# Layer 1's rows divided by their norm on ScalarE, then turned by plain transposes instead of by products with a diagonal

## The chip, the cores and the metric

The kernel runs on one core of one Trainium2 chip. The metric is the device time of one execution in microseconds (us). The median of three runs of the kernel before is 1140.3 us.

## The reference

Two residual layers act on 256 rows of width 2048. Layer 0 mixes with a gated spatial unit, layer 1 with latent attention. Both begin alike, and the change concerns how layer 1 begins:

```python
def rms_norm(x, g):
    xf = x.astype(jnp.float32)
    y = xf * lax.rsqrt(jnp.mean(xf * xf, axis=-1, keepdims=True) + NORM_EPS)
    return (y * g.astype(jnp.float32)).astype(x.dtype)
...
def reference(x, c, ada_w, ada_b, pre_g, post_g, sgu_w_in, ...):
    cond = jax.nn.silu(c)
    for i in range(DEPTH):                                  # DEPTH = 2
        mod = cond @ ada_w[i] + ada_b[i]
        shift, scale, gate = jnp.split(mod, 3, axis=-1)
        h = rms_norm(x, pre_g[i]) * (1 + scale[:, None, :]) + shift[:, None, :]
        ...
        y = sgu_mixer(h, ...) if i % N_MIXERS == 0 else mla_mixer(h, ...)   # both start with h @ w_in
        x = x + gate[:, None, :] * rms_norm(y, post_g[i])
    return x
```

Everything is float32.

## The kernel before

**Tiling.** The 256 rows are two blocks of 128, `b = 0` and `b = 1`; a block's 2048 columns are four tiles `q = 0..3` of 128 x 512. TensorE (PE) contracts over partitions, so the left operand of each product is a turned 128 x 128 piece (16 pieces, index `k`, four in each `q`). A float32 product is made of three: every operand is split into a rounded high part (`...H`, or `h` of a weight) and a remainder (`...L`, `l`), and PE sums high x high, low x high and high x low. ScalarE (ACT) makes the high part with a cast, VectorE (DVE) the low part with a subtraction. Weights stream in as tiles of 128 x 2 x 512 (`wm_0`, `wm_2`, ... for layer 1's input weights; a number is the first `k` of two), cast to `wm_..h` by ACT and subtracted to `wm_..l` by DVE.

**Order.** Each engine takes its instructions in the order in which the Python code writes them. Around the joint of the two layers this order is written out by hand in the string `PLAN`.

**The joint.** Layer 0's last matrix `po` ends with column tile 3, block 0 ahead of block 1. When block 0's sums are done, `ready1` adds the residual to the four tiles (`add`, DVE, tiles named `yg` in the trace, `x1[b][q]` in the code), squares and sums them (ACT), takes the root (ACT, tile `r`), its reciprocal (DVE, `ri`), and multiplies the identity matrix by that column: `d`, a diagonal with each row's 1/norm (DVE, `diag_of`, line 273). `turn_h1` then multiplies each 128 x 128 piece of `x1` with that diagonal on PE, which turns the piece and scales it in one product. For block 1 the same six steps lie in the list `later`, and the plan's `c1` runs one of them at a time.

**The plan's letters.** `Tbq` is `turn_h1` (four pieces into two PSUM banks, tile `h`), `Fbq` is `mod_h1` (two pieces by ACT, two by DVE: times `amul`, plus `shift`, tile `h1f`), `Hbq` the two casts to `h1H` on ACT, `Lbq` the two subtractions to `h1L` on DVE. `gN` issues N weight tiles' products for block 0, `bN` for block 1, `eN` N of layer 0's last ones (block 1), `s1` stages one weight tile (cast and subtraction), `c1` one step of `later`. The part that matters here:

```python
PLAN = "e1 e1 e1 e1 T00 T01 s1 F00 F01 H00 L00 H01 e1 e1 L01 T02 T03 g1 c1 F02 H02 c1 g1 g1 L02 s1 c1 c1 g1 c1 F03
        c1 g1 H03 g1 L03 T11 s1 T10 F11 F10 H10 L10 g1 s1 b1 H11 b1 L11 T12 F12 H12 L12 s1 T13 b1 F13 H13 ..."
```

So block 0's last `ready1` step stands just ahead of `e1 e1 e1 e1` in the code (ACT and DVE have no work in these), and block 1's last one (the sixth `c1`) between `F03` and `H03`. The four PSUM banks of the pool `pa` hold two `T` at a time, so `T02` and `T03` take the banks that `F00` and `F01` have read.

Of the kernel before, what the change touches and what calls it, by code (L numbers as in the profile page):

```python
# [8 lines left out]
F32 = mybir.dt.float32  # L9
# [6 lines left out]
P = 128  # L16
D = 2048
KD = D // P
S = 256
NB = S // P  # L20
# [134 lines left out]
def tile_trunk(  # L155
# [7 lines left out]
    nc = tc.nc  # L163
    x = x[0]
    out = out[0]
# [5 lines left out]
    sp = ctx.enter_context(tc.tile_pool(name="sp", bufs=1))  # L171
# [6 lines left out]
    def slot(name, shape=(P, 512), dt=F32):  # L178
        return sp.tile(list(shape), dt, tag="s", name=name, bufs=SLOTS)

    def small(name, n):
        return sp.tile([P, n], F32, tag="sm", name=name, bufs=16)
# [4 lines left out]
    def aux_bank(name):  # L187
        return pa.tile([P, 512], F32, tag="ax", name=name)

    def mm(o, l, r, start, stop):  # L190
        nc.tensor.matmul(o, lhsT=l, rhs=r, start=start, stop=stop)  # L191
# [12 lines left out]
    ident = const.tile([P, P], F32, name="ident")  # L204
# [49 lines left out]
    def rstd_of(ss, n, name, between=None):  # L254
        r = small(name, 1)
        nc.scalar.activation(r, ss, AF.Sqrt, bias=eps_t, scale=1.0 / n)
        if between:
            between()
        ri = small(name + "i", 1)
        nc.vector.reciprocal(out=ri, in_=r)  # L260
        return ri

    def sumsq(parts, name):
# [3 lines left out]
        t = small(name + "t", 1)  # L267
        nc.vector.reduce_sum(out=t, in_=ss, axis=AX.X)
        return t

    def diag_of(r, name):
        d = sp.tile([P, P], F32, tag="diag", name=name, bufs=4)
        nc.vector.tensor_scalar_mul(d, ident, r)
        return d


    def ada_items(name, src, width, state):
# [144 lines left out]
    def chunk_tasks(name, ks, lhs, evac, per=2):  # L422

        ps = [None, None]
        tasks = []
        ks = list(ks)
        for i in range(0, len(ks), per):
            def task(b, g, i=i):
                if i == 0:
                    ps[b] = acc_bank(f"{name}_{b}")  # L430
                h, l = g
                for j, k in enumerate(ks[i:i + per]):
                    xh, xl = lhs(k, b)
                    f = i + j == 0
                    e = i + j == len(ks) - 1
                    wh, wl = (h[j], l[j]) if isinstance(h, list) else (h[:, j, :], l[:, j, :])
                    mm(ps[b], xh, wh, f, False)
                    mm(ps[b], xl, wh, False, False)
                    mm(ps[b], xh, wl, False, e)
                if i + per >= len(ks):  # L440
                    evac(b, ps[b])

            tasks.append((lambda g, t=task: t(0, g), lambda g, t=task: t(1, g)))
        return tasks
# [288 lines left out]
    def visit(n, k0, nk):  # L733
        last = k0 + nk == KD
        ev = ev_first(n) if k0 == 0 else ev_add(n, None if not last else on_u if n < 8 else on_v)
        return chunk_tasks(f"pi_{n}_{k0}", range(k0, k0 + nk), lhs0, ev)
# [64 lines left out]
    for j, (n, k0, nk, _) in enumerate(rest):  # L801
        t = visit(n, k0, nk)
# [14 lines left out]
    def ev_z(j):  # L817
        def evac(b, ps):
            def f():
                z = slot(f"z_{j}_{b}")  # L820
                u = part[j, b]
                nc.scalar.activation(z, ps, AF.Silu)
                nc.vector.tensor_tensor(out=u, in0=u, in1=z, op=ALU.mult)
                ready.append((j, b))
            deferred.append(f)
        return evac
# [12 lines left out]
    for j in range(8):  # L839
        t = chunk_tasks(f"piz_{j}", range(KD), lhs0, ev_z(j))  # L840
# [33 lines left out]
    def ev_out(l, n, done):  # L874
        def evac(b, ps):
            def f():
                if n == 0:
                    ssy[l][b] = small(f"ssy_{l}_{b}", 4)
                nc.scalar.activation(junk, ps, AF.Square, accum_out=ssy[l][b][:, n:n + 1])
                yg[l][b][n] = slot(f"yg_{l}_{n}_{b}")  # L880
                if gates[l][n] is None:
                    nc.scalar.copy(out=yg[l][b][n], in_=ps)
                    unscaled.append((b, n))
                    return

                def gate():
                    nc.vector.tensor_tensor(out=yg[l][b][n], in0=ps, in1=gates[l][n], op=ALU.mult)

                if n < 3:
                    gate()  # L890
                else:
                    done(b, gate)

            if n == 3:
                f()
            else:
                deferred.append(f)
        return evac

    def y_rstd(l, b, gate):  # L900
        t = small(f"sst_{l}_{b}", 1)
        nc.vector.reduce_sum(out=t, in_=ssy[l][b], axis=AX.X)
        return rstd_of(t, D, f"ry_{l}_{b}", gate)

    x1 = yg[0]
    dg1 = [None, None]

    later = []

    def ready1(b, gate):  # L910
        r, ss1 = [], small(f"ss1_{b}", 4)

        def norm():
            r.append(y_rstd(0, b, gate))

        def add(q):
            y = yg[0][b][q]
            nc.vector.scalar_tensor_tensor(y, y, r[0], xr[b][q], op0=ALU.mult, op1=ALU.add)
            nc.scalar.activation(junk, y, AF.Square, accum_out=ss1[:, q:q + 1])

        def turn():
            t = small(f"ss1t_{b}", 1)
            nc.vector.reduce_sum(out=t, in_=ss1, axis=AX.X)
            dg1[b] = diag_of(rstd_of(t, D, f"r1_{b}"), f"d1_{b}")

        steps = [norm] + [lambda q=q: add(q) for q in range(4)] + [turn]
        if b == 0:
            for f in steps:
                f()
        else:  # L930
            later.extend(steps)

    lhs_y = quad_lhs(yH, yL)
    for n in range(4):
        t = chunk_tasks(f"po_{n}", range(32), lhs_y, ev_out(0, n, ready1))
# [17 lines left out]
    def turn_h1(b, q):  # L953
        ps = hp1[b][q] = [aux_bank(f"h1_{b}_{q}_{i}") for i in range(2)]
        for i in range(4):
            mm(ps[i // 2][:, (i % 2) * P:(i % 2 + 1) * P], x1[b][q][:, i * P:(i + 1) * P], dg1[b], True, True)

    def mod_h1(b, q):
        ps = hp1[b][q]
# [29 lines left out]
    def ev_lat(n):  # L989
        def evac(b, ps):  # L990
            def f():
                lat[b][n] = slot(f"lat_{b}_{n}")
                nc.scalar.copy(out=lat[b][n], in_=ps)
            deferred.append(f)
        return evac

    t = chunk_tasks("pm_0", range(KD), lhs1, ev_lat(0))
# [21 lines left out]
    def tail(n):  # L1019
        for f in later[:n]:  # L1020
            f()
        del later[:n]

    acts = dict(T=turn_h1, F=mod_h1, H=high_h1, L=low_h1)
    for w in PLAN.split():
        if w[0] in "THFL":
# [84 lines left out]
    def ev_sz(n):  # L1111
        def evac(b, ps):
            def f():
                sz[b][n] = slot(f"sz_{b}_{n}")
                nc.scalar.activation(sz[b][n], ps, AF.Silu)
            deferred.append(f)
        return evac

    t = chunk_tasks("pm_2", range(KD), lhs1, ev_sz(0))
# [5 lines left out]
    t = chunk_tasks("pm_3", range(KD), lhs1, ev_sz(1))  # L1125
# [245 lines left out]
    t = chunk_tasks("pp_2", range(KD), lhs_o, ev_out(1, 2, finish))  # L1371
# [3 lines left out]
    t = chunk_tasks("pp_3", range(KD), lhs_o, ev_out(1, 3, finish))  # L1375
# [51 lines left out]
```

## Time and profile before

| what | value |
|---|---|
| time, median of 3 runs | 1140.3 us (1138.54 to 1141.61) |
| profiled execution | 1140.05 us |
| its span, first to last instruction | 1138.3 us |
| PE busy | 1109.9 us, 98% of the span |
| DVE busy | 901.6 us, 79% |
| ACT busy | 571.3 us, 50% |
| mean granted TensorE clock | 0.998 |

The profile shows one execution, and its times of day are us from the start of the span. The profiled execution took 1.75 us more than its span. The work that changes lies between 766 us and 791 us. "Idle before" in a row is the time in which the engine did nothing ahead of this instruction, with the engine and tile that ended it. A duration of the profile reaches past the start of the next instruction of the same engine, where the two overlap; from start to start is then what one costs in a row of them.

### The profile page before, as it was taken

What the parts mean: (1) busy time and instruction counts of PE and PEld (TensorE: products, weight loads), DVE (VectorE), ACT (ScalarE), POOL (GpSimd) and SP (SyncE); (2) the same over time, 40 slices, a digit from 0 to 9 for tenths busy, and PEclk for the clock granted to TensorE, in tenths of its full rate; (3) what the DMA queues carried; (4) which work ended last, traced back from release to release, by engine and by line L of the source; (5) the groups of instructions that cost most, each with busy time, mean ns of one, the idle gap of its engine ahead of it and who ended that gap; (6) DMA issues with size and microseconds to landing.
All of it is one profiled execution on the core that took longest, in us unless ns stands there. A gap on an engine that the chain in (4) does not pass through costs nothing.

```text
span 1138.3 us, 15632 instructions
## 1 busy us (share of the span) xinstructions
PE 1109.9 (98%) x5585; PEld 940.3 (83%) x5585; DVE 901.6 (79%) x1201; ACT 571.3 (50%) x821; POOL 23.8 (2%) x51
## 2 busy tenths in 40 slices
PE   5999999999999999999999999999999999999997
PEld 4787878888887888888888888888888999999885
DVE  3889899978888898898788788857888467568765
ACT  3765434354456555554544443457574445455441
POOL 1000000000000000000001000000000000000000
PEclk9999999999999999999999999999999999999999
DMA  9999898988786987788689999973988445345672
GB/s 325 316 323 321 280 369 289 366 286 279 250 296 227 313 308 241 258 273 292 231 299 333 362 365 354 385 235 93 354 309 277 146 153 169 92 148 187 229 280 82
DMA packets 158206, 304.34 MB, mean 267 GB/s; under 512 B 12057, under 2 KB 29056, under 8 KB 158128
## 3 DMA queue, kind: packets, MB, share of 16 engines
q1 hardware_dynamic: 156128, 297.84, 76.5%
q0 software_dynamic: 1968, 5.49, 1.7%
q8 instruction: 44, 0.72, 0.2%
q14 instruction: 34, 0.28, 0.1%
q10 hardware_dynamic: 32, 0.01, 0.0%
HBM read 301.17 MB, written 2.11 MB: 266 GB/s over the span
## 4 chain that ended last, share of the span: by engine, by line
PE 81%; DVE 7%; DMA 5%; ACT 4%; issue 3%; SPq 0%; DVEq 0%; ACTq 0%
PE pi L191 18%; PE piz L191 15%; PE po L191 15%; PE pm L191 10%; PE pp L191 8%; DMA wi<-in_sgu_w_in_dram 3%; PE k L191 2%; PE v L191 2%; PE s L191 2%; PE qn L191 2%; PE o L191 1%; DMA first<-in_ada_w_dram 1%; PE mix L191 1%; DVE part L702 1%; PE qr L191 1%
## 5 line engine op out<-in xcount | busy, mean ns | idle before, releaser
L296 DVE SCALAR_TENSOR_TENSOR acc_ada<-ada,sc,acc_ada 128x1024 f32<-128x1024 f32 (+1 forms) x135 | 148.8, 1102 | 0.8
L296 DVE SCALAR_TENSOR_TENSOR acc_gate<-gate,sc,acc_gate 128x1024 f32<-128x1024 f32 x60 | 76.7, 1278 | 0.0
L702 DVE TENSOR_TENSOR part<-pi,part 128x512 f32<-128x512 f32 x92 | 59.2, 683 | 1.2 <-PE pi L191 1.2
L113 ACT CAST wi_8h<-wi 128x1024 fp32r<-128x1024 f32 x24 | 25.2, 1051 | 36.5 <-DMA wi<-in_sgu_w_in_dram 30.5
L113 ACT CAST wi_6h<-wi 128x1024 fp32r<-128x1024 f32 x24 | 25.1, 1051 | 36.4 <-DMA wi<-in_sgu_w_in_dram 30.3
L113 ACT CAST wi_4h<-wi 128x1024 fp32r<-128x1024 f32 x24 | 25.2, 1051 | 28.2 <-DMA wi<-in_sgu_w_in_dram 26.9
L114 DVE TENSOR_TENSOR wi_10l<-wi,wi_10h 128x1024 fp32r<-128x1024 f32 x24 | 29.3, 1221 | 12.1 <-ACT wi_10h L113 11.9
L114 DVE TENSOR_TENSOR wi_14l<-wi,wi_14h 128x1024 fp32r<-128x1024 f32 x24 | 29.3, 1221 | 7.0 <-ACT wi_14h L113 7.0
L114 DVE TENSOR_TENSOR wi_6l<-wi,wi_6h 128x1024 fp32r<-128x1024 f32 x24 | 29.3, 1220 | 4.2 <-ACT wi_6h L113 4.2
L114 DVE TENSOR_TENSOR wi_8l<-wi,wi_8h 128x1024 fp32r<-128x1024 f32 x24 | 29.3, 1221 | 3.8 <-ACT wi_8h L113 3.8
L114 DVE TENSOR_TENSOR wi_0l<-wi,wi_0h 128x1024 fp32r<-128x1024 f32 x23 | 28.1, 1221 | 5.2 <-ACT wi_0h L113 5.2
L114 DVE TENSOR_TENSOR wi_12l<-wi,wi_12h 128x1024 fp32r<-128x1024 f32 x24 | 29.3, 1220 | 2.7 <-ACT wi_12h L113 2.5
L114 DVE TENSOR_TENSOR wi_4l<-wi,wi_4h 128x1024 fp32r<-128x1024 f32 x24 | 29.3, 1220 | 2.1 <-ACT wi_4h L113 2.1
L113 ACT CAST wi_2h<-wi 128x1024 fp32r<-128x1024 f32 x24 | 25.2, 1051 | 11.3 <-DMA wi<-in_sgu_w_in_dram 9.2
L1271 ACT ACTIVATE sm<-sm,nm 128x128 f32<-128x128 f32 (+1 forms) x32 | 14.3, 448 | 32.4 <-DVE nm L1269 32.3
L113 ACT CAST wi_10h<-wi 128x1024 fp32r<-128x1024 f32 x24 | 25.1, 1045 | 10.8 <-DMA wi<-in_sgu_w_in_dram 10.1
L114 DVE TENSOR_TENSOR wi_2l<-wi,wi_2h 128x1024 fp32r<-128x1024 f32 x24 | 29.3, 1221 | 1.2 <-ACT wi_2h L113 1.2
L113 ACT CAST wi_0h<-wi 128x1024 fp32r<-128x1024 f32 x23 | 24.1, 1050 | 10.5 <-DMA wi<-in_sgu_w_in_dram 9.3
L113 ACT CAST wi_12h<-wi 128x1024 fp32r<-128x1024 f32 x24 | 25.2, 1049 | 5.5 <-DMA wi<-in_sgu_w_in_dram 3.6
L113 ACT CAST wi_14h<-wi 128x1024 fp32r<-128x1024 f32 x24 | 25.1, 1045 | 4.7 <-PE pi L191 2.5
L715 ACT ACTIVATE part<-part 128x512 f32<-128x512 f32 x16 | 9.9, 632 | 34.7 <-DVE part L702 34.7
L191 PE MATMUL pi<-wi_4h,hH 128*128 128x512 f32 x64 | 25.3, 396 | 1.1 <-DVE part L702 1.1
(694 smaller groups left out, 3811.1 us busy)
## 6 DMA issues: line engine op xcount, KB each, us to landing
wi<-in_sgu_w_in_dram SPq DMA_DIRECT2D x191, 512.0 KB, 5.3
ada<-in_ada_w_dram SPq DMA_DIRECT2D x240, 256.0 KB, 5.3
gate<-in_ada_w_dram SPq DMA_DIRECT2D x64, 512.0 KB, 5.4
wo<-in_sgu_w_out_dram SPq DMA_DIRECT2D x64, 512.0 KB, 6.2
wm<-in_mla_w_in_dram SPq DMA_DIRECT2D x48, 512.0 KB, 5.5
wp<-in_mla_w_out_dram SPq DMA_DIRECT2D x32, 512.0 KB, 5.3
ukv<-in_mla_w_ukv_dram SPq DMA_DIRECT2D x16, 512.0 KB, 4.6
uq<-in_mla_w_uq_dram SPq DMA_DIRECT2D x12, 384.0 KB, 3.2
```

Of the source, the lines that this page charges most:

```text
L113: self.nc.scalar.copy(out=h, in_=raw)
L114: self.nc.vector.tensor_tensor(out=l[0:rows], in0=raw[0:rows], in1=h[0:rows].bitcast(F32), op=ALU.subtract)
L191: nc.tensor.matmul(o, lhsT=l, rhs=r, start=start, stop=stop)
L296: nc.vector.scalar_tensor_tensor(acc, raw, w, acc, op0=ALU.mult, op1=ALU.add)
L702: nc.vector.tensor_tensor(out=part[n, b], in0=ps, in1=part[n, b], op=ALU.add)
L715: nc.scalar.activation(part[n, b], part[n, b], AF.Gelu)
L1271: nc.scalar.activation(sm[:, i, :], sm[:, i, :], AF.Exp, bias=nm[:, i:i + 1], scale=scale, accum_out=su[:, i:i + 1])
```

## The change

The diagonal goes. In its place ACT multiplies each of the block's four tiles `x1[b][q]` (128 x 512) by the column `ri` and writes the result to a tile of its own, `x1n[b][q]`. `turn_h1` then turns the pieces of `x1n` with PE's transpose, against the identity. For block 0 the four are written in the order 0, 1, 2, 3, for block 1 in the order 1, 0, 2, 3, which is that of `T11`, `T10`, `T12`, `T13`. `x1` itself stays as it is, since the end of the kernel adds it again. The eight new tiles come from the same pool of 53 slots as most others.

```diff
-    def diag_of(r, name):
-        d = sp.tile([P, P], F32, tag="diag", name=name, bufs=4)
-        nc.vector.tensor_scalar_mul(d, ident, r)
-        return d
...
-    dg1 = [None, None]
+
+    x1n = [[None] * 4 for _ in range(NB)]
...
         def turn():
             t = small(f"ss1t_{b}", 1)
             nc.vector.reduce_sum(out=t, in_=ss1, axis=AX.X)
-            dg1[b] = diag_of(rstd_of(t, D, f"r1_{b}"), f"d1_{b}")
+            ri = rstd_of(t, D, f"r1_{b}")
+            for q in (0, 1, 2, 3) if b == 0 else (1, 0, 2, 3):
+                x1n[b][q] = slot(f"x1n_{b}_{q}")
+                nc.scalar.mul(x1n[b][q], x1[b][q], ri)
...
     def turn_h1(b, q):
         ps = hp1[b][q] = [aux_bank(f"h1_{b}_{q}_{i}") for i in range(2)]
         for i in range(4):
-            mm(ps[i // 2][:, (i % 2) * P:(i % 2 + 1) * P], x1[b][q][:, i * P:(i + 1) * P], dg1[b], True, True)
+            nc.tensor.transpose(out=ps[i // 2][:, (i % 2) * P:(i % 2 + 1) * P],
+                                in_=x1n[b][q][:, i * P:(i + 1) * P], identity=ident)
```

**ACT's queue at the end of block 0's norm.** In the rows that follow, the digits after a tile's name are its indices (`b`, `q` and, for `h1f`, the half) and a running number; a tile's own trailing digit before the first underscore is dropped. Before:

```order
L256 ACTIVATE r_0_6652<-ss1t_6650,eps_t 128x1
L113 CAST wm_8h<-wm_8_6554 128x1024
L965 ACTIVATE h1f_0_0_6707<-h_0_0_0_6689,shift,amul 128x128 x2
L965 ACTIVATE h1f_1_0_6713<-h_0_1_0_6695,shift,amul 128x128 x2
L975 CAST h1H_0_6719<-h1f_0_0_6707 128x256
```

And with the change:

```order
L256 ACTIVATE r_0_6652<-ss1t_6650,eps_t 128x1
L923 ACTIVATE x1n_0_6656<-yg_0_0_5620,r_0i 128x512
L923 ACTIVATE x1n_1_6658<-yg_1_0_5983,r_0i 128x512
L923 ACTIVATE x1n_2_6660<-yg_2_0_6336,r_0i 128x512
L923 ACTIVATE x1n_3_6662<-yg_3_0_6633,r_0i 128x512
L113 CAST wm_8h<-wm_8_6554 128x1024
L965 ACTIVATE h1f_0_0_6713<-h_0_0_0_6695,shift,amul 128x128 x2
L965 ACTIVATE h1f_1_0_6719<-h_0_1_0_6701,shift,amul 128x128 x2
L975 CAST h1H_0_6725<-h1f_0_0_6713 128x256
```

All four products stand ahead of the cast of `wm_8` and of everything that ACT does for `F00`, `F01`, `H00` and `H01`.

**ACT's queue at the end of block 1's norm.** The same place for block 1, the sixth `c1` of the plan. Before:

```order
L965 ACTIVATE h1f_3_0_6816<-h_0_3_0_6752,shift,amul 128x128 x2
L256 ACTIVATE r_1_6824<-ss1t_6822,eps_t 128x1
L975 CAST h1H_3_6836<-h1f_3_0_6816 128x256
L975 CAST h1H_3_6836<-h1f_3_1_6817 128x256
L113 CAST wm_12h<-wm_12_6568 128x1024
L965 ACTIVATE h1f_1_0_6866<-h_1_1_0_6848,shift,amul 128x128 x2
L965 ACTIVATE h1f_0_0_6872<-h_1_0_0_6860,shift,amul 128x128 x2
```

And with the change:

```order
L965 ACTIVATE h1f_3_0_6822<-h_0_3_0_6758,shift,amul 128x128 x2
L256 ACTIVATE r_1_6830<-ss1t_6828,eps_t 128x1
L923 ACTIVATE x1n_1_6834<-yg_1_1_5986,r_1i 128x512
L923 ACTIVATE x1n_0_6836<-yg_0_1_5624,r_1i 128x512
L923 ACTIVATE x1n_2_6838<-yg_2_1_6339,r_1i 128x512
L923 ACTIVATE x1n_3_6840<-yg_3_1_6747,r_1i 128x512
L975 CAST h1H_3_6848<-h1f_3_0_6822 128x256
L975 CAST h1H_3_6848<-h1f_3_1_6823 128x256
L113 CAST wm_12h<-wm_12_6568 128x1024
L965 ACTIVATE h1f_1_0_6878<-h_1_1_0_6860,shift,amul 128x128 x2
```

Here the casts of `h1H` for block 0's last tile and of `wm_12` move behind the four products. The order of PE's instructions is the same before and after; only what its 32 turning instructions read differs. DVE loses its two `d` and keeps its order otherwise.

## Rows read from the trace of the kernel before

**Rows 1.** Page, part 1: busy time, share of the span, instructions, by engine.

```profile
PE 1109.9 (98%) x5585; PEld 940.3 (83%) x5585; DVE 901.6 (79%) x1201; ACT 571.3 (50%) x821; POOL 23.8 (2%) x51
```

**Rows 2.** Windows view to PE's end: busy PE, PEld, DVE, ACT, POOL; granted clock; DMA.

```profile
797.00:1130.00 333.00, 331.41 (x1996) 294.40 (x1994) 232.50 (x394) 168.35 (x287) 5.61 (x9) 1.00 0.61 204
```

**Rows 3.** Timeline of PE (start, us, what, idle before) at the joint.

```profile
767.29 2.02 PE L191 MATMUL h<-d,yg 128*128 128x128 f32 x16
769.07 0.48 PE L191 MATMUL po<-wo_28h,yH 128*128 128x512 f32 x1
...
771.92 1.95 PE L191 MATMUL h<-d,yg 128*128 128x128 f32 x16
773.62 0.48 PE L191 MATMUL pm<-wm_0h,h1H 128*128 128x512 f32 x1
...
782.35 2.05 PE L191 MATMUL h<-d,yg 128*128 128x128 f32 x16 [0.31 <-DVE d L273]
...
786.25 0.50 PE L191 MATMUL pm<-wm_0h,h1L 128*128 128x512 f32 x1 [0.19 <-DVE h1L L981]
...
788.88 1.95 PE L191 MATMUL h<-d,yg 128*128 128x128 f32 x16
790.58 0.48 PE L191 MATMUL pm<-wm_4h,h1H 128*128 128x512 f32 x1
```

**Rows 4.** Timeline of PE: eight plain transposes of layer 0.

```profile
426.87 1.03 PE L834 MATMUL yt<-ident,part 128*128 128x128 f32 x8
427.65 0.47 PE L191 MATMUL piz<-wi_4h,hH 128*128 128x512 f32 x1
```

**Rows 5.** Timeline of ACT: the same product on layer 0's rows, line 551.

```profile
21.02 0.70 ACT L551 ACTIVATE x<-x,rx_0i 128x512 f32<-128x512 f32 x1
21.63 0.71 ACT L551 ACTIVATE x<-x,rx_1i 128x512 f32<-128x512 f32 x1
```

**Rows 6.** Timeline of ACT at the joint.

```profile
766.53 1.04 ACT L113 CAST wm_8h<-wm 128x1024 fp32r<-128x1024 f32 x1
...
778.66 0.63 ACT L919 ACTIVATE junk<-yg 128x512 bf16<-128x512 f32 x1 [2.01 <-DVE yg L918]
...
781.49 0.29 ACT L256 ACTIVATE r<-ss1t,eps_t 128x1 f32<-128x1 f32 x1
781.67 0.70 ACT L975 CAST h1H<-h1f 128x256 fp32r<-128x256 f32 x2
782.28 1.05 ACT L113 CAST wm_12h<-wm 128x1024 fp32r<-128x1024 f32 x1
```

**Rows 7.** Timeline of DVE at the joint.

```profile
766.65 0.17 DVE L260 RECIPROCAL r_0i<-r 128x1 f32<-128x1 f32 x1 [0.36 <-ACT r L256]
...
768.74 1.36 DVE L968 TENSOR_SCALAR h1f<-h,amul,shift 128x128 f32<-128x128 f32 x4
770.04 1.43 DVE L981 TENSOR_TENSOR h1L<-h1f,h1H 128x256 fp32r<-128x256 f32 x4
772.84 0.16 DVE L902 TENSOR_REDUCE sst<-ssy 128x1 f32<-128x4 f32 x1 [1.37 <-ACT junk L879]
...
776.68 1.22 DVE L114 TENSOR_TENSOR wm_10l<-wm,wm_10h 128x1024 fp32r<-128x1024 f32 x1 [1.06 <-ACT wm_10h L113]
...
781.81 0.17 DVE L260 RECIPROCAL r_1i<-r 128x1 f32<-128x1 f32 x1 [0.72 <-ACT r L256]
...
783.36 1.23 DVE L114 TENSOR_TENSOR wm_12l<-wm,wm_12h 128x1024 fp32r<-128x1024 f32 x1 [0.39 <-ACT wm_12h L113]
...
785.78 0.98 DVE L981 TENSOR_TENSOR h1L<-h1f,h1H 128x256 fp32r<-128x256 f32 x2
```

**Rows 8.** Timeline of PE: two successive wide products shortly after PE's sparse first stretch.

```profile
31.28 0.58 PE L191 MATMUL pi<-wi_firsth,hH 128*128 128x512 f32 x1
31.69 0.40 PE L191 MATMUL pi<-wi_firsth,hL 128*128 128x512 f32 x1
```

**Rows 9.** Windows view: a stretch after PE's last product (columns as in rows 2).

```profile
1134.00:1135.00 1.00, 0.00 (x0) 0.00 (x0) 0.53 (x1) 0.00 (x0) 0.00 (x0) 0.59 0.93 350
```

## Prediction

> **What bounds the kernel now.** I read the page first, then PE's timeline at the joint of the layers, then those of ACT and DVE beside it. PE is busy for 98% of the span [rows 1], and from 797 us to its end it is idle for 1.6 us of 333 us [rows 2]. So a microsecond of PE time saved or lost at the joint reaches the end nearly whole: nothing behind the joint has slack to swallow it, and none of PE's waits there is for a transfer. What the reader must then see is who leads at the joint itself. For block 0 it is PE: its products with the diagonal at 767.29 and 771.92 start without a wait [rows 3]. For block 1 it is the chain of ACT and DVE: PE waits 0.31 us for `d` at 782.35 and again 0.19 us for `h1L` at 786.25 [rows 3]. That chain has no slack at these two points, and the change adds work to it.
>
> **What PE saves.** The 16 records from 767.29 to 769.07 are eight products with a diagonal: 1.78 us [rows 3]. The same count takes 1.70 us from 771.92 to 773.62 and from 788.88 to 790.58 [rows 3]. Eight plain transposes take 0.78 us from their start to that of the next product [rows 4]. So a pair of `T` becomes 0.92 to 1.0 us shorter, and the four pairs some 3.8 us, if nothing makes PE wait.
>
> [...]
>
> **What DVE saves.** Two small products with the identity, between the reciprocals at 766.65 and 781.81 and the next work. They cost nothing where DVE then waits for ACT's casts anyway, and I give them no price of their own: the chain below shows who needs what.
>
> **What ACT gets.** Eight products of 128 x 512 with a column. Layer 0 has the same call on the same shape: 0.70 us each, 0.61 us from start to start [rows 5]. I take 0.615, so four cost 2.46 us. They stand in ACT's queue ahead of the weight cast and of `F` and `H`, and the first waits for the reciprocal, for which no ACT work waited before. I follow both blocks, with 0.03 us from an end to the start that it releases (block 1's root ends at 781.78 [rows 6] and its reciprocal starts at 781.81 [rows 7]).
>
> **Block 0.** The reciprocal ends at 766.82 [rows 7]. The four products start at 766.85, 767.47, 768.08 and 768.70, and ACT comes to the cast of `wm_8` at 769.31 where it came at 766.53 [rows 6]: 2.78 us late. DVE's subtraction for `wm_8` waits for that cast, and DVE's half of `F00` and `F01` stands behind it, so this moves from 768.74 to 771.52, and ends at 772.88 [rows 7]. The four `h1L` move from 770.04 to 772.82 and end at 774.25.
> PE: `T00` waits for the first product, which ends at 767.56, and starts at 767.59 instead of 767.29; `T01` waits for the second and starts at 768.21; layer 0's last twelve products begin at 768.60 instead of 769.07 and take 2.85 us as before, to 771.45 [rows 3]. `T02` and `T03` need the PSUM banks that `F00` and `F01` read. The last of these is free at 772.88, so `T03` ends at 773.11, and `g1` starts there instead of at 773.62. Of the 2 us that PE saves in block 0, 0.5 is left.
>
> **What the late chain does next.** Block 1's norm starts with a sum on DVE at 772.84 [rows 7]. It now stands behind the `h1L` of block 0 and starts at 774.2, 1.34 us late. From here to the root at 781.49 [rows 6] it is one chain across both engines. It has two idle stretches, DVE's 1.06 us before `wm_10l` [rows 7] and ACT's 2.01 us before 778.66 [rows 6]; but each ends with work of the other engine that stands on this same chain (ACT's cast of `wm_10` comes behind the square of the first added tile, DVE's additions behind the subtraction for `wm_10`). So I let the 1.34 us through: the root starts at 782.83.
>
> **Block 1.** The reciprocal, 781.81 before [rows 7], runs from 783.15 to 783.32. The products start at 783.35, and the first ends at 784.06. PE has finished its 36 products for `g1` at 781.5 (782.04 before, less the 0.5 us) and now waits 2.6 us there: the saving of block 0 and that of `T11` and `T10` are lost in this wait. ACT is through its four products at 783.35 + 2.46 = 785.81, and the casts of `H03` start then instead of at 781.67 [rows 6]: 4.14 us late, of which 1.34 came from block 0, 0.34 is the new wait for the reciprocal and 2.46 the products. Behind them, all by 4.14 us: the cast of `wm_12` from 782.28 [rows 6] to 786.42, its subtraction from 783.36 [rows 7] to 787.50, both halves of `F11` and `F10`, and `h1L` of block 1 from 785.78 [rows 7] to 789.92. PE needs `wm_12`, then this `h1L`; the product that waited at 786.25 [rows 3] starts at 790.39.
>
> **After that** PE leads again, and `T12` and `T13` shrink from 1.70 to 0.78 us: 0.92 us back. Their input is long there. The casts and subtractions behind them keep their distance to PE.
>
> **The sum.** 4.14 - 0.92 = 3.22 us more. The profiled execution took 1140.05 us, so 1143.27 us; the median of the runs lies 0.25 us above that execution: 1143.5 us. This is 0.28% more. I count 0.3% (3.4 us) as what a measurement of this kernel can tell from no change, so the sum ends just below it.
>
> **Bounds of the unknown.** No row shows this product at this place. All eight count. At no overlap each costs 0.70 us as in the duration of rows 5, which adds 8 * 0.085 = 0.7 us to the sum: 1144.2. At the price of the squares around them (0.63 us with the same 0.09 us of overlap, 0.54 [rows 6]) the sum is 0.6 us smaller: 1142.9. I stay with 0.615, since it is the same instruction. The transposes are the same instruction as in rows 4, too. The new slots carry no wait of note: what used these slots last was done long before.
>
> **Rival 1: PE decides, and the saving arrives (faster).** If ACT's products ran in time that ACT has to spare, PE's 3.8 us would reach the end: 1140.3 - 3.8 = 1136.5 us. It decides from the point at which the chain of block 1 has 4.1 us to spare before 786.25. Against it: PE waits there already, for exactly this chain. For it: ACT is busy for half the span only [rows 1], so one who reads the page alone would expect it.
>
> **Rival 2: the delay of block 0 is swallowed (no change).** If the idle 2.01 us of ACT before 778.66 [rows 6] takes up the 1.34 us, block 1 costs 2.80 us, less 0.92: 1.9 us, 1142.2 us. That needs DVE's additions to come in time although their start is late, which the order of the two queues speaks against.
>
> **Rival 3: PE's clock falls in the new wait (slower).** From 781.5 to 789.7 PE would have four short waits with a few transposes and products between them. Rows show a slower pace once: after the sparse first stretch two wide products start 0.41 us apart [rows 8], against 0.23 us in the twelve that take 2.85 us [rows 3]. If eight products behind the wait went at 0.41, it would cost 8 * 0.18 = 1.4 us: 1144.9 us. [...]
> [...]
>
> **How the numbers follow.** The sum as worked out, within half a microsecond or so: 0.62; because it ends so near 3.4 us, four parts in ten of it lie beyond and six within. Rival 3: 0.13, all slower. Rival 2: 0.17, all within 0.3%. Rival 1: 0.08, faster. So faster 0.08, within 0.3% 0.37 + 0.17 = 0.54 less a little for products dearer than I took: 0.50; slower 0.42. The forecast is the first case, 1143.5 us. The range reaches from below rival 2 to above rival 3, with the scatter of a median of runs that lie 3 us apart: 1140.8 to 1145.5 us.
>
> **What the profile of the changed kernel would show.** Right: eight ACT products near 0.7 us, 0.61 apart; the cast of `wm_8` some 2.8 us and that of `wm_12` some 4.1 us later; PE idle for about 2.6 us before `T11`, ended by ACT's `x1n`, and again before the products of `wm_12`; `T12` and `T13` in 0.8 us; the first product of layer 1's second chunk about 3.2 us later; no other place changed. Wrong: PE not waiting before `T11` (rival 1); the root of block 1 at 781.5 as before (rival 2); products 0.4 us apart after 788 us (rival 3); or an end that moves by other than PE does at the joint, by which something behind it would have slack that I do not see.

## The result, and the profile after

The changed kernel takes 1145.61 us (median of 4 runs, 1145.50 to 1148.53) against 1139.92 us (median of 4, 1138.54 to 1141.61) of the kernel before beside it: ratio 1.0056, 95% interval 1.0044 to 1.0068. It is slower by 5.7 us, where 3.2 were forecast, and lies 0.1 us above the range.

The profiled execution of it is the longest of the four, 1148.53 us at a span of 1146.7 us. Its part 1 of the page answers to [rows 1]: PE has 32 instructions fewer, ACT 8 more.

```profile
PE 1112.7 (97%) x5553; PEld 939.8 (82%) x5553; DVE 901.8 (79%) x1199; ACT 576.2 (50%) x829; POOL 23.8 (2%) x51
```

ACT's timeline at the joint answers to [rows 6] (columns: start, us, what, idle before). All times of this profile are 2.75 us later than in before from ahead of the joint on: the root of block 0 stands at 769.08 us, in before at 766.33.

```profile
769.08 0.29 ACT L256 ACTIVATE r<-ss1t,eps_t 128x1 f32<-128x1 f32 x1 [0.22 <-DVE ss1t L919]
769.61 2.56 ACT L923 ACTIVATE x1n<-yg,r_0i 128x512 f32<-128x512 f32 x4 [0.23 <-DVE r_0i L260]
772.07 1.03 ACT L113 CAST wm_8h<-wm 128x1024 fp32r<-128x1024 f32 x1
...
782.71 0.63 ACT L915 ACTIVATE junk<-yg 128x512 bf16<-128x512 f32 x1 [2.01 <-DVE yg L914]
...
785.54 0.29 ACT L256 ACTIVATE r<-ss1t,eps_t 128x1 f32<-128x1 f32 x1
786.06 2.56 ACT L923 ACTIVATE x1n<-yg,r_1i 128x512 f32<-128x512 f32 x4 [0.23 <-DVE r_1i L260]
788.53 0.69 ACT L975 CAST h1H<-h1f 128x256 fp32r<-128x256 f32 x2
789.13 1.04 ACT L113 CAST wm_12h<-wm 128x1024 fp32r<-128x1024 f32 x1
```

Take off the 2.75 us: the cast of `wm_8` comes 2.79 us late (forecast 2.78), the root of block 1 at 782.79 (782.83), the casts of `H03` at 785.78 (785.81), the cast of `wm_12` at 786.38 (786.42). ACT's idle 2.01 us is still there, as the sum assumed. ACT's queue did what the prediction said it would, to 0.05 us.

PE's timeline answers to [rows 3]:

```profile
770.38 1.27 PE L955 MATMUL h<-ident,x1n 128*128 128x128 f32 x8 [0.18 <-ACT x1n L923]
...
786.83 1.70 PE L955 MATMUL h<-ident,x1n 128*128 128x128 f32 x8 [2.49 <-ACT x1n L923]
790.22 0.80 PE L191 MATMUL pm<-wm_12h,h1H 128*128 128x512 f32 x1 [1.69 <-ACT wm_12h L113]
...
792.50 0.63 PE L191 MATMUL pm<-wm_12h,h1L 128*128 128x512 f32 x1
792.93 0.63 PE L191 MATMUL pm<-wm_12l,h1H 128*128 128x512 f32 x1
793.35 0.63 PE L191 MATMUL pm<-wm_0h,h1H 128*128 128x512 f32 x1
...
794.51 0.40 PE L191 MATMUL pm<-wm_0h,h1H 128*128 128x512 f32 x1
794.74 0.40 PE L191 MATMUL pm<-wm_0h,h1L 128*128 128x512 f32 x1
...
796.59 1.04 PE L955 MATMUL h<-ident,x1n 128*128 128x128 f32 x8
```

The wait ahead of `T11` is 2.49 us (forecast 2.6), ended by ACT's `x1n`; the next ends with the cast of `wm_12`. But two rows are not as forecast: eight transposes behind the wait take 1.70 us and not 1.04, and the products behind them start 0.43 us apart until 794.2 and 0.23 us apart from 794.5 on. The windows view says why (us of the window, busy PE, PEld, DVE, ACT, POOL, granted clock, share of the DMA engines, GB/s):

```profile
784.00:786.00 2.00, 0.34 (x2) 0.00 (x0) 0.88 (x4) 1.80 (x7) 0.00 (x0) 1.00 0.43 174
786.00:788.00 2.00, 1.17 (x7) 0.97 (x8) 0.03 (x1) 1.94 (x4) 0.00 (x0) 0.88 0.00 0
788.00:790.00 2.00, 0.53 (x3) 0.13 (x1) 0.76 (x2) 2.00 (x5) 0.00 (x0) 0.50 0.04 8
790.00:792.00 2.00, 1.74 (x3) 1.00 (x4) 1.80 (x4) 1.97 (x6) 0.00 (x0) 0.50 0.01 4
792.00:794.00 2.00, 2.00 (x6) 1.54 (x5) 1.46 (x5) 1.26 (x3) 0.00 (x0) 0.50 0.61 155
794.00:796.00 2.00, 2.00 (x9) 1.60 (x9) 1.88 (x3) 0.70 (x3) 0.32 (x1) 0.91 0.28 108
```

The granted clock goes to 0.50 of full speed from 788 to 794 us and is 0.91 from 794 to 796 us; PE was busy throughout from 792 us on. This is rival 3, and the products 0.43 us apart are the sign that the prediction gave for it.

A second loss lies 60 us further on, where the prediction expected no change. The waits view of PE from 760 to 1000 us (us in total, times, longest) has two entries behind the joint, the last two here, that are new or larger. In before PE waits there 0.33 us for `cql` (the line below) and never for `acc_gate`.

```profile
PE h L955 <- ACT x1n L923: 2.7, 2, 2.5
PE pm L191 <- ACT wm_12h L113: 1.7, 1, 1.7
PE ckp L1079 <- DVE cql L1090: 0.9, 1, 0.9
PE tgate L313 <- DVE acc_gate L291: 0.8, 1, 0.8
```

```profile
854.21 0.63 PE L1079 MATMUL ckp<-ident,kvn 128*128 128x128 f32 x4 [0.33 <-DVE cql L1090]
```

**How I split the time.** How long the work ahead of the joint takes moves by up to 4 us between the profiles: block 0's root stands between 765.1 and 769.1 us in them. So I measure inside each one: the *joint* from block 0's root (ACT, `r`) to the first product of `wm_4` for block 1, called T here, which stands right behind `T13`; and the *rest* from T to the end of the span. Before: T at 790.58 [rows 3], joint 790.58 - 766.33 = 24.25 us, rest 1138.3 - 790.58 = 347.72 us. After: T at 797.39, joint 28.31, rest 349.31. So 4.06 us are lost at the joint and 1.59 us behind it, 5.65 us together; the medians are 5.7 us apart.

### The profile page after: what moved, and what is told of

Its sections match the earlier page's. It is cut to its first block, busy times and chain, and to the rows that moved or that the text cites. A ratio compares the mean times of both kernels' runs of the same rounds, so it can differ in the third digit from the quotient of the medians.

```text
span 1146.7 us, 15576 instructions
## 1 busy us (share of the span) xinstructions
PE 1112.7 (97%) x5553; PEld 939.8 (82%) x5553; DVE 901.8 (79%) x1199; ACT 576.2 (50%) x829; POOL 23.8 (2%) x51
## 4 chain that ended last, share of the span: by engine, by line
PE 58%; DVE 3%; ACT 3%; DMA 1%; issue 1%; DVEq 0%; ACTq 0%
PE piz L191 15%; PE po L191 14%; PE pm L191 8%; PE pp L191 8%; PE k L191 2%; PE v L191 2%; PE s L191 2%; PE qn L191 2%; PE o L191 1%; DMA wm<-in_mla_w_in_dram 1%; PE mix L191 1%; PE qr L191 1%; PE yt L829 1%; ACT junk L915 0%; DVE acc_gate L291 0%
```

## Experiments

The table holds the split of all profiles. Each ratio is against runs of the kernel before on the same chip, whose medians were 1139.6 to 1139.9 us. The last three columns are told under "The rest". They are counted from T; *packet* is the start of the one-microsecond window in which the DMA view shows a packet of queue q8.

| run | median us | ratio to before | joint | rest | wm_10 cast | wm_6 cast | packet |
|---|---|---|---|---|---|---|---|
| before (two profiles, times of the second) | 1139.36 | 1.0001 [0.9991, 1.0011] | 24.25, 24.24 | 347.72, 347.73 | 36.21, 36.22 | 54.02, 54.06 | 42, 41 |
| after | 1145.61 | 1.0056 [1.0044, 1.0068] | 28.31 | 349.31 | 36.32 | 55.62 | 52 |
| after again | 1145.66 | 1.0051 [1.0034, 1.0068] | 29.36 | 348.91 | 36.81 | 55.27 | 51 |
| block 0 alone | 1141.70 | 1.0016 [1.0006, 1.0026] | 25.55 | 348.36 | 36.21 | 54.69 | 46 |
| block 1 alone | 1143.02 | 1.0031 [1.0018, 1.0044] | 27.97 | 347.83 | 36.51 | 54.21 | 47 |
| after, filled | 1142.83 | 1.0028 [1.0017, 1.0039] | 27.48 | 347.67 | 36.24 | 53.95 | 45 |
| products alone | 1144.03 | 1.0035 [1.0021, 1.0048] | 29.60 | 347.38 | 36.23 | 53.76 | 42 |
| transposes alone | 1139.33 | 1.0000 [0.9991, 1.0010] | 22.36 | 348.92 | 37.30 | 55.30 | 51 |
| GpSimd for two | 1139.76 | 0.9998 [0.9989, 1.0007] | 23.36 | 348.28 | 36.68 | 54.66 | 43 |
| the same + 10 tiny | 1139.30 | 0.9998 [0.9989, 1.0007] | 23.34 | 347.34 | 36.21 | 53.68 | 42 |
| after + 44 tiny | 1145.18 | 1.0041 [1.0026, 1.0056] | 27.93 | 347.50 | 36.24 | 53.82 | 39 |
| before + 83 tiny | 1141.23 | 1.0017 [1.0007, 1.0027] | 24.25 | 347.58 | 36.21 | 53.93 | 54 |
| before + 93 tiny | 1141.90 | 1.0019 [1.0009, 1.0028] | 24.25 | 348.15 | 36.22 | 53.80 | 52 |
| before + 103 tiny | 1141.77 | 1.0016 [1.0006, 1.0026] | 24.29 | 348.58 | 36.21 | 54.88 | 50 |

### Both blocks, and each alone

**After again**, unaltered. 

> The changed kernel, unaltered, for a second profile. Theory (queue): ScalarE's products put block 1's chain 4.1 us back, which costs 3.2 us net at the joint, the fall of PE's clock costs 0.8 us more there, and some 1.6 us come 60 us later, where PE waits for sums of layer 1's gate that stand in DVE's queue behind a weight that lands late. If this last part is a consequence of the change, it recurs here (PE waits of over 1.4 us for tgate and ckp between 840 and 880 us, against 0.3 us before) and the time is again about 5.6 us above the kernel before. Rival (chance): the late weight is scatter of that one execution; then the profile shows waits below 0.5 us there and a span about 1.5 us nearer to the kernel before.

The joint came out 1.05 us longer than in the first profile of after, at the same wait of 2.49 us ahead of `T11`: the clock stood at 0.50 longer.

```profile
784.00:786.00 2.00, 0.91 (x5) 0.92 (x6) 0.16 (x1) 1.77 (x4) 0.00 (x0) 0.66 0.00 0
786.00:792.00 6.00, 4.54 (x12) 2.98 (x12) 4.03 (x9) 5.23 (x12) 0.00 (x0) 0.50 0.17 40
792.00:796.00 4.00, 4.00 (x13) 3.11 (x12) 1.90 (x3) 0.96 (x3) 0.63 (x2) 0.64 0.52 162
```

**Block 0 alone** and **block 1 alone**: the other block keeps its diagonal, here and in `turn_h1`.

```diff
             ri = rstd_of(t, D, f"r1_{b}")
+            if b != 0:                      # block 1 alone: b != 1
+                dg1[b] = diag_of(ri, f"d1_{b}")
+                return
             for q in (0, 1, 2, 3) if b == 0 else (1, 0, 2, 3):
```

> Only block 0 has the products on ScalarE and the plain transposes; block 1 keeps its diagonal. Queue theory: the first 1.34 us of the delay remain (block 1's first sum on DVE behind block 0's low parts), T12 and T13 save nothing: 1.3 us above the kernel before (ratio 1.001), PE's wait before T11 about 1.9 us in place of 0.31, clock not fallen. Rival (each block costs the same half): 2.8 us above. Rival (PE's saving arrives in block 0): 0.5 to 1 us below the kernel before.

> Only block 1 has the products and transposes. Queue theory: root of block 1 at its old place, casts of the last h1H and of wm_12 2.8 us later, T12 and T13 0.92 us shorter: 1.9 us above the kernel before (ratio 1.0017), PE waits about 0.7 us before T11 and about 2 us before wm_12's products; 0.5 us more if PE's clock falls in these. Rival (each block costs the same half): 2.8 us above.

Block 0 alone costs 1.30 us at the joint: the 1.34 us of the sum, let through whole (rival 2 is out). It has one wait of 2.06 us for `d`, and the granted clock stays at 1.00:

```profile
782.41 2.05 PE L191 MATMUL h<-d,yg 128*128 128x128 f32 x16 [2.06 <-DVE d L273]
```

```profile
780.00:784.00 4.00, 1.94 (x16) 1.59 (x15) 2.46 (x8) 3.97 (x12) 0.00 (x0) 1.00 0.22 86
784.00:788.00 4.00, 3.82 (x19) 2.78 (x18) 3.34 (x8) 3.24 (x8) 0.52 (x2) 1.00 0.48 131
```

Block 1 alone should cost 0.34 + 2.46 - 0.92 = 1.88 us and costs 3.72. Its rows and windows on PE:

```profile
781.55 1.27 PE L967 MATMUL h<-ident,x1n 128*128 128x128 f32 x8 [0.74 <-ACT x1n L932]
784.94 0.80 PE L191 MATMUL pm<-wm_12h,h1H 128*128 128x512 f32 x1 [2.12 <-ACT wm_12h L113]
```

```profile
784.00:786.00 2.00, 1.06 (x2) 0.50 (x2) 1.51 (x3) 2.00 (x5) 0.00 (x0) 0.59 0.01 4
786.00:790.00 4.00, 3.96 (x10) 3.04 (x10) 3.34 (x9) 2.65 (x6) 0.32 (x1) 0.50 0.44 131
```

So 1.84 us are left for the clock, by difference. With one wait of 2.06 us between products (block 0 alone) it stayed at 1.00; with waits of 0.74 and 2.12 us and eight transposes between them it went to 0.50.

### The waits filled with work

**After, filled**: 18 wide products whose result is overwritten stand ahead of `T11` (10) and `T10` (8), so that PE works through the wait and the queues of ACT and DVE stay as in after.

```diff
+FILL = (8, 10)
...
     def turn_h1(b, q):
         ps = hp1[b][q] = [aux_bank(f"h1_{b}_{q}_{i}") for i in range(2)]
+        if b == 1 and q < 2:
+            for j in range(FILL[q]):
+                mm(ps[j % 2], hH1[0][0][:, 0, :], held[0][1][0][0], True, True)
```

> The changed kernel with PE kept busy in its two new waits: ten and eight products of 128 x 512, whose results are overwritten at once, ahead of T11 and of T10. Nothing that ACT or DVE does moves. If the fall of PE's clock costs 0.8 us at the joint, the granted clock stays at 1.00 from 784 to 796 us, the products behind the waits start 0.23 us apart in place of 0.43, and the time is 0.8 us below the changed kernel (1.1 to 1.5 us if the late start of the later weights follows from it too). Rival (the clock costs nothing, since the chain of ACT and DVE leads there): no change against the changed kernel.

Eighteen products that nobody needs make the changed kernel faster, 1142.83 against 1145.66 us beside it, which is more than the 0.8 to 1.5 us that I had expected. Against the profile of after again the joint is 1.88 us shorter and the rest 1.24 us, so the gain is not the clock's alone. The granted clock is 1.00 from 784 to 796 us, and the joint is 3.23 us longer than before, where the sum of the prediction says 3.22.

```profile
783.41 0.66 PE L959 MATMUL h<-ident,x1n 128*128 128x128 f32 x4 [0.24 <-ACT x1n L924]
...
786.80 0.50 PE L192 MATMUL pm<-wm_12h,h1H 128*128 128x512 f32 x1 [0.44 <-ACT wm_12h L114]
...
788.06 0.50 PE L192 MATMUL pm<-wm_12l,h1H 128*128 128x512 f32 x1 [0.53 <-DVE wm_12l L115]
...
789.67 0.50 PE L192 MATMUL pm<-wm_0h,h1L 128*128 128x512 f32 x1 [0.19 <-DVE h1L L985]
```

```profile
784.00:788.00 4.00, 3.09 (x15) 2.02 (x13) 1.99 (x4) 4.00 (x9) 0.00 (x0) 1.00 0.01 2
788.00:792.00 4.00, 3.75 (x15) 2.78 (x16) 3.33 (x9) 2.52 (x6) 0.45 (x2) 1.00 0.43 131
```

### Each half of the change alone

**Products alone**: before, with the eight ACT products added (results unread) and the diagonal kept. **Transposes alone**: before, with plain transposes of the undivided rows. This leaves the division by the norm out; each transpose still waits for `d`, now a 0/1 matrix made from the reciprocal.

```diff
-            dg1[b] = diag_of(rstd_of(t, D, f"r1_{b}"), f"d1_{b}")
+            ri = rstd_of(t, D, f"r1_{b}")                     # products alone
+            dg1[b] = diag_of(ri, f"d1_{b}")
+            for q in (0, 1, 2, 3) if b == 0 else (1, 0, 2, 3):
+                nc.scalar.mul(slot(f"x1n_{b}_{q}"), x1[b][q], ri)
```

```diff
-        nc.vector.tensor_scalar_mul(d, ident, r)              # transposes alone
+        nc.vector.tensor_scalar(out=d, in0=ident, scalar1=r, scalar2=0.0, op0=ALU.mult, op1=ALU.is_gt)
...
-            mm(ps[i // 2][...], x1[b][q][:, i * P:(i + 1) * P], dg1[b], True, True)
+            nc.tensor.transpose(out=ps[i // 2][...], in_=x1[b][q][:, i * P:(i + 1) * P], identity=dg1[b])
```

> Before, with the eight products on ScalarE added in the place where the change puts them, written to buffers that nobody reads; the turns stay products with the diagonal. Queue theory (what is lost is lost by ACT's queue alone): the casts of wm_8 and wm_12, the norm of block 1 and h1L come as late as in after, T12 and T13 give nothing back: joint +4.1 us against before, 1143.9 us when PE's clock stays at full speed. Clock theory: PE now has shorter gaps (about 1.5 us ahead of T11 and of the products of wm_12) with products and not transposes between; if the clock falls all the same, another 0.8 to 1.9 us, 1144.7 to 1145.8 us. If the products cost nothing and the loss came from the transposes: 1139.8 us.

> Before, with plain transposes of the rows that are not divided by their norm (the division is left out), each still waiting for d, which is made as a 0/1 matrix out of the reciprocal; no products on ScalarE. So PE's saving of 3.8 us stands alone. Queue theory: blocks 0's 1.8 us, and the 0.9 us of T11 and T10, end in PE's waits for d and for h1L, which come when they came before; only T12 and T13 give 0.9 us: 1138.9 us, with a wait of about 2.1 us ahead of T11. If PE decided, 1136.0 us. Clock theory: if that wait makes the clock fall, 0.8 to 1.9 us are added: 1139.7 to 1140.8 us.

The products alone lengthen the joint by 5.35 us: the 4.14 us of the queue, and 1.21 us that I put down, by difference, to the clock, which fell here too (0.68 and 0.50 in the two stretches of 2 us from 788 us on), although PE does the same products as before and waits at most 1.77 us at a time. So the clock fell here without a transpose, with the waits that ACT's queue brings (1.61, 1.77 and 0.53 us), and with the waits filled and the transposes in place it stayed at 1.00.

The transposes alone shorten the joint by 1.89 us, of 3.8 us that PE saves, and behind waits of 1.22, 0.53 and 0.16 us the products start 0.23 us apart, as in before. I had forecast 0.92, from `T12` and `T13`. The rest comes from block 0: layer 0's last twelve products end about 1 us earlier, ACT's square of their result is what block 1's norm starts from, and so `d` comes 0.97 us earlier against block 0's root. In the changed kernel this gain is hidden behind the products (the norm then waits for DVE). Only half of what PE saves could be had at this place with no price at all; and of these 1.89 us, 1.20 are lost again in the rest, most of them (1.09) ahead of the cast of `wm_10` in the table.

**GpSimd for two**: before, with `T12` and `T13` alone as transposes; GpSimd, which has been idle for 162.13 us there, divides their rows.

```diff
+            if b == 1:
+                for q in (2, 3):
+                    x1n[q] = slot(f"x1n_{b}_{q}")
+                    nc.gpsimd.tensor_scalar_mul(x1n[q], x1[b][q], ri)
...
+            if b == 1 and q >= 2:
+                nc.tensor.transpose(out=ps[i // 2][:, (i % 2) * P:(i % 2 + 1) * P],
+                                    in_=x1n[q][:, i * P:(i + 1) * P], identity=ident)
+                continue
```

> Before, with only T12 and T13 (block 1) as plain transposes; their rows are divided by the norm on GpSimd, which has nothing to do there. Queue theory: no queue on the path gets work, the two products are done before PE comes to T12 at 788.9 us: 0.9 us less than before, 1138.9 us. Rival: GpSimd takes over 3 us for a product of 128 x 512, or holds up DVE's work beside it: T12 waits for it, 1140 to 1143 us.

The two products take 3.87 us on GpSimd and are done by 785.8 us, before PE wants them. The joint is 0.89 us shorter (0.92 forecast), but the rest is 0.56 us longer, and the time is that of before within what the runs can tell.

### The rest

**Before again.** 

> The kernel before, unaltered, for a second profile of it. Both theories: ratio 1.000. What differs is the stretch from block 1's last T to the end of the span, which was 347.72 us in the first profile of before and 349.31, 348.91, 348.36, 347.83 and 347.67 us in those of after, of after again, of block 0 alone, of block 1 alone and of the filled one. If that part (0 to 1.6 us) is scatter in the landing of the weight wm_6, this second profile may lie anywhere from 347.6 to 349.4 us, and wm_6 is cast at another distance from the T than the 54.0 us of the first. If the change itself causes it, it lies at 347.7 +- 0.2 us, with PE's wait for cql at 0.3 us as before.

The second profile of before has the rest to 0.01 us as the first. In all profiles ACT waits, some 50 us behind T, for several weights in a row, longest for `wm_4` and `wm_6` (3.83 and 1.84 us in before), whose transfers are under way at a busy share of the 16 DMA engines of 0.96 (836 to 845 us in before) and 0.99 (846 to 853 us in after). The row for `wm_6` in before, and in after:

```profile
844.60 1.05 ACT L113 CAST wm_6h<-wm 128x1024 fp32r<-128x1024 f32 x1 [1.84 <-DMA wm<-in_mla_w_in_dram]
```

```profile
853.01 1.05 ACT L113 CAST wm_6h<-wm 128x1024 fp32r<-128x1024 f32 x1 [3.61 <-DMA wm<-in_mla_w_in_dram]
```

From T these are 54.02 and 55.62 us: 1.60 us, and the rest is 1.59 us longer. In the table the rest follows this cast almost one to one, and the waits of PE for `acc_gate` and `cql` are what stands behind it in DVE's queue. The transfers are issued at the same distance from T in both, to 0.13 us. What differs in the views is a packet of 16 KB (on the page 44 are 0.72 MB) of the queue that the page lists as "q8 instruction". It comes 42 us behind T in before, ahead of these transfers, and 52 us behind T in after, amid them. The DMA view of after, from 849 to 851 us (queue: packets, MB, share of 16 engines):

```profile
q1 hardware_dynamic: 328, 0.67, 94.1%
q8 instruction: 1, 0.02, 2.9%
```

In the page's counts a transpose is one PE and one PEld instruction where a diagonal product is two of each, so the change makes PE's program shorter by 32 such pairs (5553 against 5585). That this shifts such packets was my estimate; in the table the packet comes at 41 to 42 us with as many pairs as in before, at 43 with 8 fewer, at 45 to 47 with 14 to 16 fewer, at 51 to 52 with 32 fewer. To test this I moved them with tiny transposes at the program's start, where PE waits for its first transfers (3.29 us for `rows_c` in before), and nothing else:

```diff
+    for _ in range(44):
+        nc.tensor.transpose(out=pc[0:16, 128:144], in_=ident[0:16, 0:16], identity=ident[0:16, 0:16])
     nc.tensor.transpose(out=pc[:, 0:16], in_=rows_c[0:16, :], identity=ident[0:16, 0:16])
```

> After, with 44 tiny transposes (16 x 16, overwritten) at the start of the program, where PE waits for its first transfers anyway: nothing at the joint changes, but PE's instruction stream is longer, so the 16 KB packet of the instruction queue (q8 in the page's part 3) that lands 53 us behind the last T of block 1 in after comes some 9 us earlier against it, at 42 to 45 us, where before has it. Code theory (that packet, between the packets of wm_4 and wm_6, makes wm_6 land 1.2 to 1.6 us late): wm_6 is cast 54.0 us behind that T, and the rest of the span is 347.7 us, as in before; 1144.2 us. Scatter theory: 55.3 to 55.6 us and 348.9 to 349.3 us as in both profiles of after; 1145.6 us. The joint is 28.3 to 29.4 us long in both, and the start may be up to some us later.

> Before, with 83 of the same tiny transposes at the start: the start of the program may come up to 15 us later, which is read apart; what counts is the distance from the last T of block 1 on. The instruction packet that lies 42 us behind that T in before comes to lie near 52 us, as in after. Code theory: wm_6 is cast 55.2 to 55.6 us behind the T and the rest of the span is 348.9 to 349.3 us, though nothing at the joint was changed. Scatter theory: 54.0 and 347.7 us as in both profiles of before. The joint is 24.25 us long in both.

> Before with T12 and T13 as plain transposes of rows that GpSimd divides by the norm, and ten tiny transposes more at the start, which move the instruction packet from 43.8 us behind the last T to some 41.6 us, ahead of the burst of transfers, as in before. Code theory: wm_6 is cast at 54.0 us and the 0.9 us of the joint arrive: 1138.7 us, ratio 0.9992. Scatter theory: as in the run without the ten, 54.7 us and 1139.4 us. The joint is 23.4 us long in both.

In after, 44 of them moved the packet from 52 to 39 us behind T, `wm_6` was cast at 53.82, and the rest fell from 349.31 and 348.91 to 347.50 us. With GpSimd for two, ten brought the rest from 348.28 to 347.34 us, but the packet moved by one window only, and 0.47 us of the gain is there at `wm_10` already, ahead of the packet; the time stayed that of before. The third run missed its place: 83 put the packet at 54 us, behind the landing of `wm_6`, and the rest is that of before. So I ran the kernel before with ten and with twenty more:

> Before with 93 tiny transposes at the start instead of 83. With 83 the instruction packet came 54 to 55 us behind the last T of block 1, when wm_6 had landed; ten more move it some 3 us forward, to 51 to 52 us, where after, after again and the transposes alone have it. Code theory: wm_6 is cast 55.2 to 55.6 us behind the T and the rest of the span is 348.9 to 349.3 us, at an unchanged joint of 24.25 us; against the run with 83, 1.3 to 1.7 us longer. Rival (the late landing belongs to what the change does at the joint): 53.9 and 347.6 us as with 83.

> The same with 103: the packet at 48 to 49 us. Code theory: wm_6 is cast late too, 54.6 to 55.6 us, the rest of the span 348.3 to 349.3 us. Rival: 53.9 and 347.6 us.

With 103 the packet lies at 50 us, `wm_6` is cast at 54.88 and the rest is 1.00 us longer than with 83, at a joint that nobody touched. With 93 it lies at 52 us, `wm_6` comes in time (53.80), but the next weight is awaited for 1.03 instead of 0.29 us and the rest is 0.57 us longer. The rows for both weights with 103 (the first wait, 2.82 us, was 2.21 us with 83):

```profile
847.50 1.05 ACT L113 CAST wm_6h<-wm 128x1024 fp32r<-128x1024 f32 x1 [2.82 <-DMA wm<-in_mla_w_in_dram]
848.86 1.05 ACT L113 CAST wm_8h<-wm 128x1024 fp32r<-128x1024 f32 x1 [0.31 <-DMA wm<-in_mla_w_in_dram]
```

(The roots of block 0 stand at 766.7 to 768.3 us in these three, so some 1 to 2 us of their longer times are the start.)

Not all of the loss arises at this place. The cast of `wm_10` lies ahead of the packet in every profile, and in four it is already late against T: by 0.60 us in after again, 1.09 in the transposes alone, 0.47 in GpSimd for two and 0.30 in block 1 alone. Before, and transposes alone (T at 788.18):

```profile
826.79 1.03 ACT L113 CAST wm_10h<-wm 128x1024 fp32r<-128x1024 f32 x1
```

```profile
825.48 1.04 ACT L113 CAST wm_10h<-wm 128x1024 fp32r<-128x1024 f32 x1
```

Why it is late there is not shown. From this cast to that of `wm_6` it takes 17.5 to 18.0 us in eleven profiles. It takes longer in four, with the packet at 46 to 52 us: 19.30 in after, 18.46 in after again, 18.48 in block 0 alone and 18.67 in before with 103. It does not with the packet at 45 and 47 us (after, filled; block 1 alone), nor at 51 us (transposes alone).

So the packet among the transfers is a likely cause of 0.6 to 1.5 us in those four, and of some 0.6 us at the next weight with 93, but it is not shown to be the cause. Each figure is one profile. The three runs with tiny transposes and a short rest (44, 83, ten) were on one chip and the two with a longer one (93, 103) on another. The ratios with 83 and 103, 1.0017 and 1.0016, do not tell the 1.0 us apart. Nor do the timed runs of after with 44 more: they scatter from 1142.73 to 1146.12 us, the profiled one is among the short ones (span 1141.0), and the median is only 0.4 us below that of after. Which of the transfers the packet must meet, the views don't show.

No version beat the kernel before by more than its measurement can tell.

## Why the prediction was wrong

**ACT's price and the chains of both blocks** were right in every step, to about 0.1 us: 2.46 us for four products, 2.78 us at the cast of `wm_8`, 1.34 us through the norm of block 1, 4.14 us at the cast of `wm_12`, PE's saving lost in a wait of 2.5 us. The sum of 3.22 us is what the joint loses when PE's clock stays up (3.23, filled).

**The first step that failed** is the low chance of rival 3, a fall of the granted clock in the new waits, the longest of them forecast at 2.6 us. In before the clock stays at 1.00 from PE's last product, which ends at 1129.98 us, to 1134 us and is 0.59 in the next microsecond [rows 9]. That shows when the clock fell once, after PE's work had ended; it doesn't show how little rest is enough. The runs: no fall with one wait of 2.06 us (block 0 alone), a fall to 0.50 with 0.74 and 2.12 us (block 1 alone), with 1.61, 1.77 and 0.53 (products alone), and in both profiles of after and in that with 44 tiny transposes more. With the waits filled it did not fall, and the joint came out at the queue's sum. The price, against the queue's sum, is 0.84 and 1.89 us in after, 0.46 with 44 more, 1.84 and 1.21 in the halves. Rival 3 had put 1.4 us on it, so the fall and its size were there, and a chance of 0.13 was the error. In the first profile of after 0.50 was granted from 788 to 794 us, with PE busy for 0.53, 1.74 and 2.00 us of each 2 us, and 0.91 in the 2 us behind these; what brings the clock back is not shown.

**The second step** is "none of PE's waits there is for a transfer", and with it that casts and subtractions behind the joint "keep their distance to PE". PE's own waits name DVE, but DVE's stand behind ACT's, and ACT's at 844.60 us end with a landing. PE already waits 0.33 us there in before, for `cql`, a row that the prediction leaves out. In after `wm_6` is cast 1.60 us later against T, and the rest is 1.59 us longer. What makes the weight late stays open: the packet is likely, not shown. That a late transfer there would reach PE at once, I could have read. Either step alone would have left the time inside the range, at some 1144.0 (queue and clock, from 1139.92) or 1144.7 us (queue and rest); both together left it by 0.1 us.

**Rivals 1 and 2.** The saving did not arrive, and could not have: alone it is worth 1.89 us at the joint and nothing in the time (1139.33 against 1139.55 us). The delay of block 0 was not swallowed: block 0 alone costs 1.30 us.

**The account.** After: 3.22 (queue) + 0.84 (clock) + 1.59 (rest) = 5.65 us; after again: 3.22 + 1.89 + 1.19 = 6.30 us, 0.60 of the last term being lost ahead of the cast of `wm_10`; the medians say 5.7 and 5.9. The forecast held the first term only. The clock's term is a difference in each case; that it is the clock is shown by the filled run, with a joint 3.23 us longer than before at a granted clock of 1.00.

## What to carry to other kernels

Before work is moved off the busiest engine, ask whose queue it joins and who stands behind it there: eight products on a half-idle engine (ACT, 50% busy) cost more than thirty-two on a full one (PE, 98%) gave back, since they stood in front of the casts that PE waits for. Do not take a wait of PE to be too short to lower its clock because one longer wait did not: here the granted clock fell to about 0.5 with one wait of 1.95 us, and with two of 0.74 and 2.12 us, and stayed at 1.00 with one of 2.06 us, and the products behind a fall started 0.43 us apart in place of 0.23. And where PE hardly waits at all, follow the few short waits back through the other queues to a transfer or not, before calling a stretch free of transfers.

## What was not expected of the hardware

- The granted clock fell to 0.50 with no single wait of PE over 2.5 us, and, in the products alone, none over 1.8 us. In the first profile of after it fell another time, far from the change, behind a single wait of 1.95 us for DVE's `part`, with no other wait of PE in the 5 us ahead of it, and PE's products then started 0.43 us apart in place of 0.23, at a granted clock of 0.52. So here a single wait stands ahead of the fall, and what decides between this one and the 2.06 us of block 0 alone is not shown.

```profile
171.77 0.47 PE L191 MATMUL pi<-wi_4h,hH 128*128 128x512 f32 x1 [1.95 <-DVE part L697]
```

```profile
170.00:173.00 3.00, 1.23 (x5) 1.05 (x6) 3.00 (x4) 1.05 (x1) 0.00 (x0) 1.00 0.95 307
173.00:176.50 3.50, 3.50 (x10) 2.72 (x9) 3.50 (x4) 2.07 (x2) 0.00 (x0) 0.52 1.03 374
```

- In the first profile of before the granted clock is 1.00 throughout from 165 to 176.5 us, with a wait of 1.12 us for the same tile, so this fall may be part of the 2.75 us by which the profile of after is late at the joint.
- Eight transposes last 1.03 us at a granted clock of 1.00 [rows 4] and 1.70 us at a mean of 0.70 (786.83 us in after).
- The page lists 44 packets of queue q8, 0.72 MB in all. With 44 tiny transposes more at the start, one of them came at 39 us behind T in place of 52 us, some 800 us later in the run. Why it moves, and what the packets carry, no view shows. In four profiles a packet amid a burst of weights went with landings 0.6 to 1.5 us late, in three, with it at 45, 47 and 51 us, it did not.
- A product of 128 x 512 with a column took 1.9 us on GpSimd (3.87 us for two) and 0.615 us from start to start on ACT, and no delay of DVE's work beside it shows at the joint: PE's wait for `h1L` is 0.19 us with ten tiny transposes more, as in before [rows 3].
